# The scheduler's model behind a 2-layer hybrid backbone kernel: default model against timeline model

## The chip, the cores and the metric

The kernel runs on one NeuronCore of one Trainium2 chip. The metric is the device time of one execution in microseconds (us). Before the change it is 2091.67 us, the median of three runs (2090.68, 2091.67 and 2097.0 us). One further execution was profiled. Engines are called TensorE (PE in the profile, PEld for its weight loads), VectorE (DVE), ScalarE (ACT), GpSimd (POOL) and SyncE (SP, which only issues DMAs).

## The reference

Two layers work on 512 latent tokens and 256 context tokens of width 1024, all in float32.

```
for layer in range(2):
    h, hc = modulate(rms_norm(x), ...), modulate(rms_norm(ctx), ...)
    layer 0: y, yc = even_mixer(...)   # 8 heads global attention (2 kv heads, qk-norm, rotary)
                                       # + 8 heads sliding-window attention with a sink; then @ w_out
    layer 1: y = odd_mixer(...)        # 8 heads 2-D neighbourhood attention with a position bias
                                       # + 8 heads RWKV-7 in both directions; then @ w_out
    x = x + g1 * y;   x = x + g2 * swiglu(modulate(rms_norm(x), ...))
    ctx gets the same after layer 0 only
return rms_norm(x)
```

The RWKV-7 part is a recurrence over tokens, `S = S * w - (S kk) (kk a)^T + v k^T`, read out as `S r`. Its initial state comes from running the same recurrence over the context tokens. The feed-forward width is 2816.

## The kernel before, in words

**Tiling.** Features lie on the 128 partitions, tokens along the free dimension. Every projection keeps float32 accuracy by three passes (`mm3`, L387 to L389): each weight tile arrives by a DMA issued on SyncE (`wraw`, L133, 512 KB), ScalarE rounds it into `whi` (L143), VectorE or, in some stages, GpSimd subtracts to get `wlo` (L145), and TensorE multiplies high by high, high by low and low by high, 24 matmuls of 512 columns for one 128x1024 weight tile against the latent tokens.

**Stages in order of time.** Layer 0's input projection (`even_in`, `even_q`), its attention (`attend` and `pair`, L587 to L667) with the context's output projection and feed-forward beside it (`ctx_rest`), then layer 0's output projection and feed-forward for the latent tokens (`onto`, `ffn`) with layer 1's context part beside them (`ctx_chain`), then layer 1. Layer 1 begins with its projections (`odd_qkv` with L978 to L998, `shift_tile` with L1102 to L1109), beside which the RWKV operands are prepared (`prepare`). Each piece of `prepare` is a chain over ScalarE, VectorE and TensorE (`rwkv_elem`, L1188 to L1230), and each of its two groups ends with a 32x32 triangular inverse on VectorE (`rwkv_inverse`): four transposes of 32x1024 (L1255), 31 elimination steps (L1259, L1262), four transposes back (L1267). The recurrence then runs in chunks of 32 tokens, both directions together (`rwkv_step`, L1311 to L1351), with the rest of `prepare` and, later, the neighbourhood attention (`odd_pair`, L1047 to L1071) beside it. Layer 1's feed-forward (L387 to L389, L420, L712, L713) and the last norm (L1672) close the kernel.

**What sets the order.** Python generators (`aside`, `step`) interleave a main and a side stream when the program is traced; constants such as `B1`, `L1` or `F1` say how many side steps go with one main step. That gives each instruction a place in the traced program, and this place is its priority (`high_priority` in `attend` and `odd_pair` moves the score matmuls `QK_AHEAD` = 30 places forward). When the TileContext closes, the scheduler plays the program through on a model of the machine: whenever an engine is free in the model, it takes the instruction of lowest place among those whose inputs and buffers are ready in the model. The order so found is fixed in the program. On the chip each engine takes its own instructions in just this order, and a semaphore wait at the head of an engine's list holds all that stands behind it. Which buffer of a pool a tile gets, and the order of DMA issues on SyncE and GpSimd, come out of the same play. Nothing of the model is left in the program but the order, the buffers and the waits that follow from them.

In the program before, VectorE has 92% of its instructions at another place than the traced one, ScalarE 87%, SyncE 83%, GpSimd 74% and TensorE 57%; in the last eighth of TensorE's instructions the order is the traced one throughout.

The functions around the change:

## Time and profile before

| what | value |
|---|---|
| median of three runs | 2091.67 us |
| profiled execution, its own time | 2095.34 us |
| its span, first to last instruction | 2093.4 us |
| TensorE busy | 1981.8 us (95%) |
| VectorE busy | 1229.4 us (59%) |
| ScalarE busy | 893.1 us (43%) |
| GpSimd busy | 247.4 us (12%) |
| mean granted TensorE clock | 0.967 |
| DMA moved | 272.66 MB, 130 GB/s |

Busy time is the union of an engine's records. Matmuls overlap in the pipeline, so a TensorE that is always busy may still be doing little per microsecond; the granted clock says at which share of its full speed it ran. A row of the waits names the waiting instruction, the instruction that released it, the total in us, how often, and the longest one. A row of the timeline gives start, duration, engine, line, operation, output and inputs, and in brackets the idle time just before it with what ended it. A row of the stages gives the stretch, its length, busy us and number of instructions for TensorE's matmuls, its weight loads, VectorE, ScalarE and GpSimd, then the granted clock, the busy share of the DMA engines and GB/s.

### The profile page before, as it was taken

What the parts mean: (1) busy time and instruction counts of PE and PEld (TensorE: products, weight loads), DVE (VectorE), ACT (ScalarE), POOL (GpSimd) and SP (SyncE); (2) the same over time, 40 slices, a digit from 0 to 9 for tenths busy, and PEclk for the clock granted to TensorE, in tenths of its full rate; (3) what the DMA queues carried; (4) which work ended last, traced back from release to release, by engine and by line L of the source; (5) the groups of instructions that cost most, each with busy time, mean ns of one, the idle gap of its engine ahead of it and who ended that gap; (6) DMA issues with size and microseconds to landing.
All of it is one profiled execution on the core that took longest, in us unless ns stands there. A gap on an engine that the chain in (4) does not pass through costs nothing.

```text
span 2093.4 us, 38293 instructions
## 1 busy us (share of the span) xinstructions
PE 1981.8 (95%) x15556; PEld 1611.0 (77%) x15556; DVE 1229.4 (59%) x2407; ACT 893.1 (43%) x1682; POOL 247.4 (12%) x366
## 2 busy tenths in 40 slices
PE   6999999999988999999999999889899989999997
PEld 4766778999986888787777776667667768888887
DVE  5756676666666443559445655775766774333335
ACT  3335557775733433552222355535345443222222
POOL 1111100000000010000112132322322120000000
PEclk9999999999999999999999998988889999999999
DMA  7353322444484445433434323455675133232321
GB/s 272 124 200 122 142 91 81 142 126 127 135 271 160 151 156 151 140 108 107 146 102 132 111 71 92 123 158 161 162 222 144 33 121 101 92 101 91 101 92 49
DMA packets 112655, 272.66 MB, mean 130 GB/s; under 512 B 15424, under 2 KB 48736, under 8 KB 110944
## 3 DMA queue, kind: packets, MB, share of 16 engines
q1 hardware_dynamic: 100256, 224.74, 34.4%
q0 software_dynamic: 12224, 45.49, 6.6%
q8 instruction: 122, 2.00, 0.4%
q14 instruction: 53, 0.43, 0.1%
HBM read 238.20 MB, written 31.98 MB: 129 GB/s over the span
## 4 chain that ended last, share of the span: by engine, by line
PE 74%; DVE 11%; issue 9%; DMA 2%; ACT 2%; POOL 1%; SPq 0%; DVEq 0%; POOLq 0%; ACTq 0%
PE ps_b L387 16%; PE ps_b L389 16%; PE ps_b L388 16%; PE ps_v L637 4%; PE ps_a L587 2%; PE ps_e L609 2%; PE ps_w L1311 2%; PE ps_w L1317 2%; PE ps_s L1340 1%; DVE kb L1262 1%; PE ps_w L1330 1%; DVE kb L1255 1%; DVE pi L1259 1%; PE ps_a L1047 1%; PE ps_e L1218 1%
## 5 line engine op out<-in xcount | busy, mean ns | idle before, releaser
L143 ACT CAST whi<-wraw 128x1024 fp32r<-128x1024 f32 (+2 forms) x291 | 292.7, 1008 | 669.8 <-PE ps_b L388 509.4
L145 DVE TENSOR_TENSOR wlo<-wraw,whi 128x1024 fp32r<-128x1024 f32 (+2 forms) x251 | 296.1, 1180 | 213.5 <-ACT whi L143 207.5
L387 PE MATMUL ps_b<-hxh,whi 128*128 128x512 f32 (+1 forms) x1040 | 402.4, 390 | 13.0 <-ACT cj L978 7.2
L388 PE MATMUL ps_b<-hxl,whi 128*128 128x512 f32 (+1 forms) x1040 | 397.8, 385 | 1.6 <-DVE hxl L380 1.5
L389 PE MATMUL ps_b<-hxh,wlo 128*128 128x512 f32 (+1 forms) x1040 | 397.3, 384 | 0.3 <-DVE wlo L145 0.2
L387 PEld LDWEIGHTS ps_b<-hxh,whi 128*128 128x128 f32 x1040 | 198.6, 192 | 60.6 <-ACT cj L978 7.8
L388 PEld LDWEIGHTS ps_b<-hxl,whi 128*128 128x128 f32 x1040 | 199.0, 192 | 40.1 <-DVE hxl L380 3.0
L389 PEld LDWEIGHTS ps_b<-hxh,wlo 128*128 128x128 f32 x1040 | 198.7, 192 | 39.6 <-DVE wlo L145 1.3
L387 PE MATMUL ps_b<-act,whi 128*128 128x512 f32 (+1 forms) x570 | 200.5, 352 | 4.6 <-ACT whi L143 2.8
L389 PE MATMUL ps_b<-act,wlo 128*128 128x512 f32 (+1 forms) x570 | 197.0, 346 | 1.5 <-DVE wlo L145 1.5
L388 PE MATMUL ps_b<-act,whi 128*128 128x512 f32 (+1 forms) x570 | 196.7, 345 | 0.6 <-DVE act L124 0.6
L387 PE MATMUL ps_b<-hch,whi 128*128 128x256 f32 x552 | 159.6, 289 | 0.1
L389 PE MATMUL ps_b<-hch,wlo 128*128 128x256 f32 x552 | 156.2, 284 | 0.4 <-DVE wlo L145 0.4
L388 PE MATMUL ps_b<-hcl,whi 128*128 128x256 f32 x552 | 155.9, 283 | 0.0
L387 PEld LDWEIGHTS ps_b<-act,whi 128*128 128x128 f32 x570 | 109.5, 192 | 22.7 <-issue 5.5
L389 PEld LDWEIGHTS ps_b<-act,wlo 128*128 128x128 f32 x570 | 109.6, 192 | 15.0 <-DVE wlo L145 2.1
L388 PEld LDWEIGHTS ps_b<-act,whi 128*128 128x128 f32 x570 | 109.6, 192 | 12.9 <-DVE act L124 1.0
L420 DVE SCALAR_TENSOR_TENSOR xx<-ps_b,mod,xx 128x512 f32<-128x512 f32 (+1 forms) x64 | 43.7, 684 | 120.6 <-PE ps_b L389 119.3
L145 POOL TENSOR_TENSOR wlo<-wraw,whi 128x1024 fp32r<-128x1024 f32 (+1 forms) x40 | 88.5, 2217 | 204.6 <-ACT whi L143 180.0
L713 DVE TENSOR_TENSOR ff_a<-ff_a,ps_b 128x512 f32<-128x512 f32 x44 | 30.2, 687 | 134.3 <-PE ps_b L389 133.6
L387 PEld LDWEIGHTS ps_b<-hch,whi 128*128 128x128 f32 x552 | 104.7, 190 | 5.7 <-issue 2.5
L389 PEld LDWEIGHTS ps_b<-hch,wlo 128*128 128x128 f32 x552 | 104.4, 190 | 1.7 <-DVE wlo L145 1.4
(373 smaller groups left out, 3470.6 us busy)
## 6 DMA issues: line engine op xcount, KB each, us to landing
wraw<-in_ffi SPq DMA_DIRECT2D x132, 512.0 KB, 3.5
xx<-in_wmod POOLq DMA_DIRECT2D x48, 512.0 KB, 5.0
wraw<-in_w1in SPq DMA_DIRECT2D x43, 512.0 KB, 3.6
wraw<-in_ffo SPq DMA_DIRECT2D x48, 448.0 KB, 3.3
wmod<-in_wmod POOLq DMA_DIRECT2D x32, 512.0 KB, 4.8
wraw<-in_ffo SPq DMA_DIRECT2D x24, 512.0 KB, 3.5
op<-op SPq DMA_DIRECT2D x32, 384.0 KB, 4.2
qx<-in_wmod SPq DMA_DIRECT2D x16, 512.0 KB, 6.7
```

The costliest lines, as they stand in the source:

```text
L143: self.nc.scalar.copy(hi[:, 0:n], raw)
L145: e.tensor_tensor(lo[:, 0:n], raw, hi[:, 0:n].bitcast(F32), op=ALU.subtract)
L387: mm(out, lhsT=wh, rhs=hh, start=first, stop=False)
L388: mm(out, lhsT=wh, rhs=hl, start=False, stop=False)
L389: mm(out, lhsT=wl, rhs=hh, start=False, stop=last)
L420: self.nc.vector.scalar_tensor_tensor(X[:, m, c], ps[:, 0:n][:, c], gate[:, m, i : i + 1], X[:, m, c], op0=ALU.mult, op1=ALU.add)
L587: nc.tensor.matmul(o, lhsT=q, rhs=k[:, b : b + o.shape[1]], start=i == 0, stop=i == len(passes) - 1)
L609: nc.tensor.transpose(pt[:, P * (j - c) : P * (j - c) + P], p[:, P * j : P * j + P], self.ident)
L637: self.nc.tensor.matmul(ps[HD * u : HD * u + HD, col : col + P], lhsT=vs[u][j], rhs=pts[u][:, j, :], start=j == 0, stop=j == nk - 1, tile_ ...
L713: V.tensor_tensor(a, a, pg[1][:, 0:w], op=ALU.mult)
L1311: mm(wy[HD * u + HD - W_ + r : HD * u + HD, p, :], lhsT=G[top[u], p, r:W_], rhs=VU[top[u], p, u, :], start=p == 0, stop=False, skip_group_ ...
L1317: mm(o, lhsT=AR[:, p, :], rhs=Sd[:, p, u, :], start=False, stop=not lat, skip_group_check=True)
```

## The change

The TileContext is opened with `schedule_with_timeline_sim=True`. The play through the program then runs on the timeline model, in which each instruction is a list of timed events that take and free devices (sequencers, engines, their queues, DMA engines), in place of the default model. The traced program, its places, the buffers' sizes and the work of every instruction stay as they are; what may differ is the order on every engine and on every DMA queue, the buffer that a tile gets, and the waits.

```
-    with tile.TileContext(nc) as tc:
+    with tile.TileContext(nc, schedule_with_timeline_sim=True) as tc:
         with ExitStack() as ctx:
             Net(ctx, tc, ins, out).run()
```

## The prediction

> **What bounds the kernel now.** I read the page first, then the stages, then TensorE's waits in the worst stage, then the timeline around the three longest of them.
>
> ```profile
> span 2093.4 us, 38293 instructions
> PE 1981.8 (95%) x15556; PEld 1611.0 (77%) x15556; DVE 1229.4 (59%) x2407; ACT 893.1 (43%) x1682; POOL 247.4 (12%) x366
> ```
>
> TensorE is the bound: 2093.4 - 1981.8 = 111.6 us of its span are idle, and no other engine passes 59%. An order changes no instruction's work, so what can move is this idle time, and the time in which TensorE runs at a lower clock. The stages say where both lie (stretch, length, busy us of PE, PEld, DVE, ACT, POOL, granted clock, DMA share, GB/s):
>
> ```profile
> 0.00:50.00 50.00, 30.06 (x271) 21.63 (x272) 25.66 (x62) 18.33 (x34) 5.92 (x8) 0.93 0.79 284
> 50.00:300.00 250.00, 239.07 (x2128) 178.94 (x2127) 163.50 (x422) 115.48 (x290) 36.91 (x62) 0.99 0.40 138
> 300.00:560.00 260.00, 258.42 (x2254) 242.85 (x2253) 177.37 (x376) 180.89 (x366) 4.95 (x5) 1.00 0.37 117
> 560.00:700.00 140.00, 127.52 (x853) 110.74 (x854) 88.31 (x194) 55.52 (x93) 10.73 (x26) 0.94 0.63 208
> 700.00:1150.00 450.00, 445.69 (x3097) 354.55 (x3095) 230.85 (x356) 161.54 (x256) 37.58 (x78) 1.00 0.42 131
> 1150.00:1560.00 410.00, 367.53 (x3629) 283.57 (x3625) 280.90 (x544) 181.81 (x354) 114.36 (x141) 0.89 0.46 135
> 1560.00:1680.00 120.00, 118.44 (x1437) 87.00 (x1433) 84.08 (x184) 57.84 (x131) 22.94 (x38) 1.00 0.39 105
> 1680.00:1750.00 70.00, 62.96 (x358) 53.64 (x359) 49.08 (x98) 34.21 (x56) 13.97 (x10) 0.95 0.34 106
> 1750.00:2060.00 310.00, 310.00 (x1369) 256.68 (x1369) 110.27 (x119) 82.65 (x101) 0.00 (x0) 1.00 0.29 92
> 2060.00:2093.40 33.40, 22.11 (x181) 21.38 (x179) 19.34 (x57) 4.79 (x10) 0.00 (x0) 0.89 0.19 63
> ```
>
> Three kinds of stage. The first 50 us (19.94 idle) and the last 33.4 us (11.29 idle) are start and end, with little to choose from. The stages 300 to 560, 700 to 1150, 1560 to 1680 and 1750 to 2060 are full: 1.58 + 4.31 + 1.56 + 0 = 7.45 us idle in 1140, so a new order can only lose there. The stage from 1150 to 1560, where layer 1's projections and the RWKV work are interleaved, holds 410 - 367.53 = 42.47 us idle, and its clock of 0.89 stands for another (1 - 0.89) x 410 = 45.1 us, or 45.1 x 367.53 / 410 = 40.4 us on the busy part. That is where an order can win. What ends TensorE's waits there:
>
> ```profile
> PE ps_b L387 <- ACT cj L978: 7.2, 3, 5.2
> PE ps_e L1218 <- DVE kb L1202: 7.0, 1, 7.0
> PE ps_e L1227 <- DVE G L1222: 7.0, 6, 2.2
> PE ps_a L1047 <- DVE sm_m L1052: 5.0, 1, 5.0
> ```
>
> The longest single waits of rows one, two and four (5.15, 7.01 and 4.98 us, 17.14 in all) can be taken apart in the timeline. The first:
>
> ```profile
> 1347.28 0.50 ACT L1196 ACTIVATE KA<-th,half 128x256 f32<-128x256 f32 x1
> 1350.98 0.42 ACT L1200 ACTIVATE P<-sg 128x256 f32<-128x256 f32 x1 [3.20 <-DVE sg L1197]
> ...
> 1354.92 0.42 ACT L1200 ACTIVATE P<-sg 128x256 f32<-128x256 f32 x1 [1.52 <-DVE sg L1197]
> 1355.25 1.09 ACT L978 ACTIVATE cj<-ps_b 128x512 f32<-128x512 f32 x1
> ...
> 1356.39 0.80 PE L387 MATMUL ps_b<-hxh,whi 128*128 128x512 f32 x1 [5.15 <-ACT cj L978]
> ```
>
> ScalarE's order has two exponentials (L1200) ahead of the eviction L978. Both wait for VectorE's scan, 3.20 and 1.52 us, and L978, whose matmuls were over by 1356.39 - 5.15 = 1351.24, waits behind them, and TensorE for its bank. The order fits a play in which the scan comes sooner than on the chip. The second:
>
> ```profile
> 1383.64 7.67 DVE L1267 STREAM_TRANSPOSE G<-kb 32x1024 f32<-32x1024 f32 x4
> 1385.55 2.35 POOL L145 TENSOR_TENSOR wlo<-wraw,whi 128x1024 fp32r<-128x1024 f32 x1 [6.44 <-ACT whi L143]
> 1384.58 0.49 PE L387 MATMUL ps_b<-hxh,whi 128*128 128x512 f32 x1 [1.19 <-ACT cj L998]
> 1392.09 1.97 PE L1218 MATMUL ps_e<-AR,kb 64*64 64x64 f32 x32 [7.01 <-DVE kb L1202]
> 1394.76 0.77 PE L388 MATMUL ps_b<-hxl,whi 128*128 128x512 f32 x1
> ```
>
> TensorE's order has L1218 behind the first of 24 matmuls of a projection. L1218 needs L1202, which sits behind four transposes of 7.67 us; the other 23 matmuls, whose last operand `wlo` is there at 1385.55 + 2.35 = 1387.90, stand behind L1218 until 1394.76. This too fits a play with shorter transposes. The third:
>
> ```profile
> 1522.30 7.69 DVE L1267 STREAM_TRANSPOSE G<-kb 32x1024 f32<-32x1024 f32 x4
> 1530.02 0.42 DVE L1341 TENSOR_TENSOR S<-ps_s,S 128x256 f32<-128x256 f32 x1
> 1531.26 1.19 PE L1047 MATMUL ps_a<-ck,cq 128*128 128x512 f32 x2 [4.98 <-DVE sm_m L1052]
> ```
>
> Here everything hangs on VectorE, which again runs four transposes in one piece; recurrence (L1341) and attention (L1052) both wait for it.
>
> **The change, part by part.** It adds and removes no work. It gives every engine and DMA queue another order.
>
> *What a nearer model recovers.* If the new play has VectorE's times about right, the first wait shrinks to L978's own 1.09 us (5.15 - 1.09 = 4.06 saved), the second to 1387.90 - 1385.08 = 2.82 us (the wait began 7.01 before 1392.09; 4.19 saved). The third stays: the transposes come ahead by their place in the program, which no model alters. So (4.06 + 4.19 + 0) / 17.14 = 0.48 of what I could take apart. For the stage: 0.48 x 42.47 = 20.4 us. Bounds: nothing, if the timeline model misses the same durations, and all 42.47.
>
> *The clock.* A long wait is paid twice:
>
> ```profile
> 1357.84 0.63 PE L387 MATMUL ps_b<-hxh,whi 128*128 128x512 f32 x1
> 1362.62 0.39 PE L387 MATMUL ps_b<-hxh,whi 128*128 128x512 f32 x1
> ```
>
> After the first wait matmuls took 0.63 us, five us later 0.39. Of the 40.4 us I take half of the share of the idle time, 40.4 x 0.48 / 2 = 9.7 us, since a wait cut to 2.8 us need not spare the slow stretch behind it. Bounds 0 and 40.4.
>
> *What the new order loses elsewhere.* The full stages are where the present order happens to keep TensorE fed. The nearest row for an ordinary interleaved stage is that from 50 to 300, with 10.93 idle in 250, or 4.4%. I put this on the two stages where attention interleaves with something else: 0.044 x 260 - 1.58 = 9.8 and 0.044 x 120 - 1.56 = 3.7, together 13.5 us. Not on 700 to 1150 and 1750 to 2060: there TensorE has dense projections whose order leaves little choice. What covers these is the work of ScalarE and VectorE done ahead (both under 71% busy in 300 to 560); without cover the price is that of 1150 to 1560, 42.47 / 410 = 10.4% idle and 11% of clock on 260 us, or 27 - 1.6 + 28.6 = 54. Bounds 0 and 54.
>
> *ScalarE's table loads* move with the order as well.
>
> ```profile
> L712 ACT ACT_TABLE_LOAD x15 | 19.2, 1283 | 1.5 <-PE ps_b L389 1.2
> L599 ACT ACT_TABLE_LOAD x14 | 18.0, 1283 | 0.2
> L712 ACT ACTIVATE xx<-ps_b 128x256 f32<-128x256 f32 x22 | 8.4, 382 | 0.2
> ```
>
> From 300 to 560 the context's 22 Silu alternate with the attention's Exp, at 15 + 14 loads of 1.283 us. Every Silu in a gap of its own would make 44 loads, 15 more, or 19.2 us of ScalarE, which has 260 - 180.89 = 79.1 us idle there. I cost this at nothing, with 0 to 19.2 as bounds. The Trainium skill, ScalarE: Activation LUTs, section "Table sets: the hidden batching unit", asks that calls be batched by set, against which an order by readiness goes; its section "What ACT_TABLE_LOAD costs" gives about 2.66 us for a switch with its drain. By that figure the 15 would be an estimated 40 us, still inside the idle time, and the sum would be the same.
>
> *Sum.* 2095.3 (the profiled execution; its span and 1.9 us around it) - 20.4 - 9.7 + 13.5 = 2078.7; the profiled execution is 3.7 above the median, so **2075 us**, 0.8% below the median.
>
> **The rivals.**
>
> *Slower: the attention stage comes apart.* Place: 300 to 560. TensorE there takes score matmuls, transposes and value matmuls that each wait for a softmax step, among the context's projections; if the new play believes a softmax step early, TensorE stands before a transpose with projections ready behind it, as at L1218 above. Price: half of the 54 us, 27, while nothing is recovered from 1150 to 1560. 2095.3 + 27 - 3.7 = 2119 us. It decides from the point where it costs more than the recovered 30. For it: 0.6% idle is little to start from. Against it: nothing in this stage takes as long on VectorE as the transposes.
>
> *Slower: SyncE's queue.* Stores wait in it for their data:
>
> ```profile
> SPq L1486 <- ACT KT L1223: 39.5, 9, 8.2
> ```
>
> ```profile
> wraw<-in_w1in SPq DMA_DIRECT2D x43, 512.0 KB, 3.6
> L143 ACT CAST whi<-wraw 128x1024 fp32r<-128x1024 f32 (+2 forms) x291 | 292.7, 1008 | 669.8 <-PE ps_b L388 509.4
> ```
>
> If the new order puts a weight fetch straight behind such a store, the weight is late by up to 8.2 us. Two weights in hand cover 2 x 24 matmuls at 310 / 1369 = 0.226 us each (the stage from 1750), 10.9 us; the wait, the landing, the rounding and GpSimd's subtraction take 8.2 + 3.6 + 1.0 + 2.4 = 15.2. So up to 4.3 us late, nine times, 39 us; half of it is 19, with nothing recovered: 2095.3 + 19 - 3.7 = 2111 us. Against it: today's order has the same queue and waits of this kind do not show on TensorE.
>
> *No change.* The orders differ, but where TensorE is full they make no difference and in 1150 to 1560 VectorE's long transposes hold in any order; 2092 us.
>
> **How the numbers follow.** Forecast 0.46, attention stage 0.27, SyncE 0.10, no change 0.17. A measurement of this kernel tells about 0.3% (6 us) from no change. That makes 0.46 faster, 0.17 the same, 0.37 slower. The forecast's own range is 2040 (all of 0.48 of both terms recovered, 39.8, and half of the 12.5 idle from 560 to 700 and 8.4 of clock, with no loss: 2095.3 - 39.8 - 10.5 - 3.7 = 2041) to 2085. With the other side taken in, and the attention stage at up to three quarters of its full price (2132), the range is 2040 to 2133.
>
> **What would show it.** Right: from 1150 to 1560 the idle time falls to about 22 us, the clock rises above 0.91, L978 no longer stands behind L1200, and the projection's matmuls run during the transposes. The losses show as idle time over 3 us in 300 to 560 and 1560 to 1680. Wrong: idle time from 1150 to 1560 at 42 us or above with the same waits for L1202 and L978, which would say that the timeline model is no nearer there; or TensorE's waits for Exp or for `sm_t` from 300 to 560 at more than 15 us.

## The result and the profile after

The kernel with the timeline model's order takes 2180.07 us (median of four runs, 2176.28 to 2183.54), the kernel before 2092.16 us beside it: a ratio of 1.0416 with a 95% interval of 1.039 to 1.0442, or 88 us slower. The prediction said 2075 us, with a range from 2040 to 2133.

The page of the kernel after, first lines:

```profile
span 2179.8 us, 38326 instructions
PE 2023.5 (93%) x15556; PEld 1644.5 (75%) x15556; DVE 1219.6 (56%) x2407; ACT 898.4 (41%) x1684; POOL 242.1 (11%) x366
```

TensorE has the same 15556 instructions. It sits idle for 2179.8 - 2023.5 = 156.3 us, 44.7 more than before, and is busy 2023.5 - 1981.8 = 41.7 us longer with the same work. About half of the loss is thus no idle time at all. The mean granted clock fell from 0.967 to 0.949. The clock's records in the two traces are either full or half, and TensorE is busy at half clock for 110.8 us before and for 170.8 us after. If a busy microsecond at half clock loses half at most, the clock accounts, as an estimate from these figures, for at most 30 of the 41.7 us; the other 12 or more are something else.

The stretches of the kernel after, at the cuts used before (length, busy us of PE, PEld, DVE, ACT, POOL, granted clock, DMA share, GB/s). Since the work falls behind more and more, a stretch holds somewhat earlier work than the stretch of the same times before:

```profile
50.00:300.00 250.00, 226.45 (x1969) 171.01 (x1963) 144.78 (x386) 102.51 (x258) 32.83 (x60) 0.95 0.36 126
300.00:560.00 260.00, 255.28 (x2087) 229.00 (x2088) 170.50 (x373) 167.90 (x352) 4.48 (x6) 0.99 0.33 107
560.00:700.00 140.00, 131.27 (x879) 115.41 (x879) 76.77 (x144) 59.03 (x95) 6.92 (x17) 0.94 0.57 191
700.00:1150.00 450.00, 431.21 (x2753) 340.09 (x2753) 228.55 (x389) 167.40 (x267) 27.91 (x65) 0.98 0.43 134
1150.00:1560.00 410.00, 378.08 (x3251) 299.90 (x3251) 256.02 (x470) 176.37 (x316) 104.51 (x124) 0.90 0.38 113
1560.00:1680.00 120.00, 105.98 (x1535) 81.10 (x1533) 86.76 (x195) 56.05 (x134) 27.21 (x51) 0.86 0.66 185
```

The stages that were full are no longer so: 700 to 1150 has 18.79 us idle where 4.31 were, 50 to 300 has 23.55 where 10.93 were.

Where the loss arises is read better from the same work in both traces. The rows below are lines of TensorE with their first and last start, first of the kernel before:

```profile
L587 PE MATMUL ps_a<-kst,qc x64: 276/362/388, 181.1 to 273.9; 128*128 128x256 f32 x64
L637 PE MATMUL ps_v<-sm_t,vt x800: 272/273/324, 186.1 to 572.8; 128*64 128x128 f32 x160
L1150 PE MATMUL ps_e<-c_blk,cj x32: 170/251/272, 1221.5 to 1250.6; 128*128 128x2 f32 x32
L1349 PE MATMUL ps_w<-VU,op x512: 214/219/316, 1407.7 to 1650.7; 128*32 128x64 f32 x128, 32*32 32x64 f32 x43
```

and of the kernel after:

```profile
L587 PE MATMUL ps_a<-kst,qc x64: 274/282/581, 196.7 to 294.7; 128*128 128x256 f32 x64
L637 PE MATMUL ps_v<-sm_t,vt x800: 272/273/476, 201.2 to 606.8; 128*64 128x128 f32 x160
L1150 PE MATMUL ps_e<-c_blk,cj x32: 165/251/252, 1289.3 to 1319.4; 128*128 128x2 f32 x32
L1349 PE MATMUL ps_w<-VU,op x512: 213/219/317, 1487.9 to 1742.8; 128*32 128x64 f32 x128, 32*32 32x64 f32 x43
```

The first attention score comes 15.6 us later, the last value product of layer 0 34.0, the first L1150 67.8, the last recurrence step (L1349) 92.1, and the end 86.4. The loss is not in one place: it grows from milestone to milestone up to the end of the recurrence, and shrinks by some 6 us behind it.

How far an order overtakes can be counted in the program: the lead of an instruction is the number of places it stands ahead of the oldest instruction of its engine that has not been issued. On TensorE the mean lead is 16.5 before and 63.1 after (largest 1059 and 2301), on VectorE 6.9 and 14.0, on ScalarE 3.2 and 8.8. One weight tile is 24 matmuls.

### The profile page after: what moved, and what is told of

Its sections match the earlier page's. It is cut to its first block, busy times and chain, and to the rows that moved or that the text cites. A ratio compares the mean times of both kernels' runs of the same rounds, so it can differ in the third digit from the quotient of the medians.

```text
span 2179.8 us, 38326 instructions
## 1 busy us (share of the span) xinstructions
PE 2023.5 (93%) x15556; PEld 1644.5 (75%) x15556; DVE 1219.6 (56%) x2407; ACT 898.4 (41%) x1684; POOL 242.1 (11%) x366
## 4 chain that ended last, share of the span: by engine, by line
PE 78%; DVE 8%; DMA 5%; issue 5%; ACT 3%; SPq 0%; POOL 0%; DVEq 0%; ACTq 0%; POOLq 0%
PE ps_b L387 16%; PE ps_b L389 16%; PE ps_b L388 16%; PE ps_v L637 4%; PE ps_a L587 2%; PE ps_e L609 2%; DMA xx<-in_wmod 2%; PE ps_s L1340 1%; PE ps_w L1311 1%; PE ps_b L465 1%; PE ps_w L1317 1%; PE ps_b L467 1%; PE ps_b L466 1%; PE ps_e L1218 1%; DMA wmod<-in_wmod 1%
## 5 line engine op out<-in xcount | busy, mean ns | idle before, releaser
L145 POOL TENSOR_TENSOR wlo<-wraw,whi 128x1024 fp32r<-128x1024 f32 (+1 forms) x40 | 88.0, 2205 | 177.7 <-ACT whi L143 156.3
L388 PEld LDWEIGHTS ps_b<-hcl,whi 128*128 128x128 f32 x552 | 104.2, 189 | 0.7 <-DVE ps_a L590 0.2
```

The costliest lines, as they stand in the source:

```text
L145: e.tensor_tensor(lo[:, 0:n], raw, hi[:, 0:n].bitcast(F32), op=ALU.subtract)
L388: mm(out, lhsT=wh, rhs=hl, start=False, stop=False)
```

## The experiments

The orders are exchanged in this way: the program is built once with one model, its order is read, and a second build with either model gets edges without semaphores between neighbours of one engine, which bind chosen engines (or places) to that order. The core of all experiments, with `build` holding what `kernel` did before:

```diff
+    def build(timeline, hold=None, engines=(), part=None, lead=None):
...
+        with tile.TileContext(nc, schedule_with_timeline_sim=timeline) as tc:
...
+                for i in hold:
+                    e = str(insts[i].engine).split(".")[-1]
+                    if e in engines and (part is None or part(i, mark)):
+                        if e in last:
+                            tc.add_manual_dep(insts[i], insts[last[e]].name, info, reason="held order")
+                        last[e] = i
+    _, hold = build(False)
```

Below, ALL stands for the five engines' names. The expectations name the theories by letters; A is that the far overtaking itself costs, the others are said where they come up.

**Is it the order at all?** The timeline play with the default's order on all engines:

```diff
+    nc, _ = build(True, hold, ALL)
```

> The timeline play, with the instructions of all five engines bound to the order that the default play gives (edges without a semaphore between neighbours of one engine). Only the buffers that tiles get and the waits may still differ from the kernel before. Theory A (the loss lies in the order) and theory B (the same, but in the order of VectorE and ScalarE): 2092 us within 10. Theory C (the loss lies in buffers, waits and what follows from them): above 2130 us.

2098.47 us beside 2094.06, ratio 1.002 (1.0002 to 1.0038). The order makes the loss; what else the other play could change (buffers, waits), together with the binding edges, is worth at most 0.4%.

**Which engine's order?** The default's order on TensorE alone, then on VectorE and ScalarE alone, each with the timeline play for the rest; then the reverse, the default play with TensorE held to the timeline's order:

```diff
+    nc, _ = build(True, hold, ("PE",))
+    nc, _ = build(True, hold, ("DVE", "Activation"))
+    _, hold = build(True)
+    nc, _ = build(False, hold, ("PE",))
```

> The timeline play, TensorE alone bound to the default order; the other engines and the DMA queues are ordered by the timeline play around it. Theory A (TensorE takes the side stream's dense matmuls too early and has none left to cover the chains): most of the 88 us come back, 2090 to 2115 us. Theory B (VectorE's and ScalarE's own orders delay the chains): little comes back, above 2150 us.

> The timeline play, VectorE and ScalarE bound to the default order, TensorE, GpSimd and the queues free. Theory A: the dense matmuls still run early where their inputs allow it, above 2140 us. Theory B: 2090 to 2115 us. If both engines only follow one another (bound evictions and roundings hold TensorE's matmuls back as well), both e2 and e3 come back.

> The reverse of the second: the default play, TensorE alone bound to the order that the timeline play gives. Theory A: most of the loss appears, 2150 to 2190 us. Theory B: little of it, 2090 to 2120 us.

Ratios 1.03 (1.0185 to 1.0415), 1.0546 (1.0489 to 1.0602) and 1.0546 (1.0479 to 1.0613); 2157.23, 2208.7 and 2208.79 us. The default's order on TensorE alone gives back some 23 of the 88 us (two executions, 18 us apart), and the two other mixtures are slower than the timeline's order whole. By the letter of the expectations the first speaks for theory B, the second for theory A, and the third lies beyond both. The question was put wrongly: these mixtures show that one engine's order can't be judged beside orders of the other engines that it was not made with.

**Which layer?** The default's order held for layer 0's places, then for layer 1's:

```diff
+    nc, _ = build(True, hold, ALL, lambda i, mark: i < mark)
+    nc, _ = build(True, hold, ALL, lambda i, mark: i >= mark)
```

> The timeline play; all engines bound to the default order for what is traced before layer 1 is called (layer 0 with layer 1's context part), free behind it. If the loss is a sum over stages as the matmuls' progress in the two traces says (68 us behind by the first matmul of layer 1's key norm, L1150, 88 at the end): about 2092 + 20 = 2112 us. If one stage's order carries the loss of the other: below 2100 or above 2135 us.

> The reverse: layer 0 free, all engines bound to the default order from layer 1's call on. Sum over stages: about 2092 + 68 = 2160 us. If layer 1's share was only a consequence of layer 0's order: 2180 us.

2116.65 us, ratio 1.0116 (1.0087 to 1.0146), and 2162.12 us, ratio 1.0334 (1.0286 to 1.0382), beside 2092.58. Layer 1 in the timeline's order costs 24 us and layer 0 costs 70; together 94, against 88 for both. Within these intervals the losses add.

**Is far overtaking what costs?** A bound on the lead: block b of an engine's instructions, in traced order, may issue only when all of block b - 2 has.

```diff
+    nc, _ = build(True, lead={"PE": 48, "DVE": 12, "Activation": 6})
+    nc, _ = build(True, lead={"PE": 150, "DVE": 30, "Activation": 20})
```

> The timeline play with a bound on how far an instruction may overtake earlier traced ones of its own engine: 48 to 96 places on TensorE (two to four weight tiles), 12 to 24 on VectorE, 6 to 12 on ScalarE. Theory A (far overtaking costs): most comes back, 2095 to 2125 us. Theory D (the play's beliefs at short range cost, a wait at the head of the line, and overtaking only fills gaps): as slow as the changed kernel or slower, 2180 us or more.

> The same with a bound of 150 to 300 places on TensorE, 30 to 60 on VectorE, 20 to 40 on ScalarE. Theory A: between the short bound and the changed kernel, 2110 to 2160 us. Theory D: within 10 us of the changed kernel's 2180.

2241.74 us, ratio 1.0714 (1.0683 to 1.0745), and 2173.77 us, ratio 1.0389 (1.0359 to 1.042). At first this seemed to end theory A. The control shows that it doesn't: the same bounds on the default play.

```diff
+    nc, _ = build(False, lead={"PE": 48, "DVE": 12, "Activation": 6})
+    nc, _ = build(False, lead={"PE": 150, "DVE": 30, "Activation": 20})
```

> Control for the short bound: the default play with the same bounds on the lead (48 on TensorE, 12 on VectorE, 6 on ScalarE). It tells whether the bound itself or the timeline play under the bound made the 2242 us. Theory D (the two plays believe different things ready at short range, and the timeline play's beliefs fit the chip worse): 2090 to 2120 us, since the default play overtakes little and the bound takes little from it. Theory A' (the block bound itself costs, whatever the play): 2150 us or more.

> Control for the long bound: the default play with 150, 30 and 20. Theory D: 2085 to 2100 us. Theory A' (the bound itself costs): 2120 us or more.

2239.32 us, ratio 1.0697 (1.0677 to 1.0716), and 2119.94 us, ratio 1.013 (1.0099 to 1.016). Of the two theories in these expectations, D is out and A' holds (the long bound just at the edge of its range): the bound itself costs the default play 146 and 27 us, so it is no clean test of theory A. What the four experiments do show: some overtaking is needed (forbidding it costs more than the whole change), and the two plays differ by 2 us under the short bound, 54 under the long one and 88 without a bound. The difference lies in what the timeline play does with its freedom to overtake.

**The traced places or the play?** The constants of the interleaving were set with the default play. If they mislead the timeline play, it should do better with the default's own order as its places:

```diff
+            def instruction_hook(self, instruction):
...
+                    self.cur_priority = places[len(here[0].instructions)]
...
+    nc, _ = build(True, places=[nth.get(i, i) for i in range(len(first) + 4000)])
```

> The timeline play, but each instruction's place is its rank in the default play's order instead of its traced place. In this play an instruction leaves that order only where the model believes its inputs or buffers late. Theory D (beliefs on what is ready): the order stays far from the default's, and the time stays within 10 us of 2180. Theory F (the traced places, tuned by hand to the default play, mislead the timeline play): 2095 to 2130 us, since the places are now the good order itself.

2175.71 us, ratio 1.0373 (1.0345 to 1.0401). Its TensorE still stands at another place than the default's order in 9409 of 12030 instructions; with the traced places it is 9449. So the places are not the cause; since the play takes the lowest place that is ready, it must take other instructions to be ready. Which of the model's durations are to blame is not shown by any run.

**The prediction's own two waits.** The default's order with L978 ahead of the two exponentials on ScalarE, and the other 23 matmuls of the projection tile ahead of the products L1218 on TensorE:

```diff
+    hold.remove(acts[k])
+    hold.insert(hold.index(acts[to]), acts[k])
...
+    moved = [i for i in pes[k:] if line[i] in (387, 388, 389)][:23]
...
+    at = hold.index(pes[k])
+    hold[at:at] = moved
+    nc, *_ = build(False, hold, ALL)
```

> The default play's order with the two edits that the prediction priced: ScalarE's L978 ahead of the two exponentials, and the other 23 matmuls of the projection tile ahead of the 16 products L1218. The prediction's first term: 4.06 + 4.19 us saved, and up to as much again in clock, so 2076 to 2084 us. Rival (the 23 matmuls are the cover of later waits, those of L1227 and of the recurrence, and are missing there): within 0.2% of the kernel before or slower, 2088 to 2100 us, with new waits of several us for L1222 and L1202 behind the moved tile.

2090.81 us beside 2093.43, ratio 0.9994 (0.9974 to 1.0015): no difference that can be measured. The two waits did go for the most part. TensorE's two waits, and the stretches around them, first of the kernel before and then of this one:

```profile
1348.95 0.50 PE L387 MATMUL ps_b<-hxh,whi 128*128 128x512 f32 x1 [0.76 <-ACT cj L978]
1389.38 1.15 PE L1218 MATMUL ps_e<-AR,kb 64*64 64x64 f32 x32 [2.07 <-DVE kb L1202]
```

```profile
1340.00:1365.00 25.00, 19.85 (x78) 14.98 (x78) 24.19 (x49) 10.20 (x19) 4.76 (x2) 0.86 0.48 136
1365.00:1382.00 17.00, 15.49 (x71) 12.63 (x70) 16.18 (x27) 7.17 (x8) 7.45 (x3) 1.00 0.47 144
1382.00:1400.00 18.00, 9.66 (x92) 7.25 (x91) 12.27 (x17) 4.80 (x10) 2.35 (x1) 0.72 0.63 207
1400.00:1450.00 50.00, 48.76 (x687) 35.39 (x687) 32.62 (x68) 29.49 (x66) 13.91 (x20) 0.87 0.47 129
```

```profile
1340.00:1365.00 25.00, 22.84 (x102) 17.42 (x101) 24.15 (x49) 12.71 (x21) 8.17 (x3) 1.00 0.39 108
1365.00:1382.00 17.00, 10.60 (x41) 7.88 (x40) 16.01 (x32) 6.08 (x8) 4.98 (x2) 0.80 0.46 139
1382.00:1400.00 18.00, 15.11 (x148) 11.73 (x148) 13.09 (x18) 5.59 (x13) 2.40 (x1) 0.81 0.65 210
1400.00:1450.00 50.00, 50.00 (x676) 37.64 (x673) 32.81 (x67) 30.48 (x67) 14.38 (x21) 0.73 0.50 134
```

The waits shrank from 5.15 to 0.76 and from 7.01 to 2.07 us, 9.33 together, a little more than predicted. About half of that came back at once as idle time elsewhere: from 1340 to 1450 TensorE is idle for 16.24 us before and 11.45 here. The stretch from 1365 has 6.40 us idle where it had 1.51, and the longest wait that is left for L978 is 4.7 us:

```profile
PE ps_b L387 <- ACT cj L978: 6.3, 3, 4.7
```

VectorE is busy for 40.16 of the first 42 us, as before (40.37), which fits a piece that it bounds, but no run here varies VectorE's work. The rival in the expectation has the time right and not the mechanism: the waits for L1222 and L1202 did not grow. And the other half was no loss in the execution that was profiled: its last L1188 starts 5.9 us earlier than before and its span is 5.8 us shorter (2087.6 to 2093.4). The twelve executions scatter from 2080 to 2106 us, the lowest with a clock of 0.970, the highest with 0.961, and their median is only 2.6 us lower. So the runs exclude the expected 2076 to 2084 us; a gain of up to 5 us they leave open.

**One part at a time.** The timeline play's order for one range of places, the default's for all others: up to the first attention score; from there to the last value product; from there to layer 1; and from layer 1's first neighbourhood score to the end.

```diff
+    nc, *_ = build(True, hold, ALL, lambda i, mark: i >= scores)
+    nc, *_ = build(True, hold, ALL, lambda i, mark: not scores <= i < onto)
+    nc, *_ = build(True, hold, ALL, lambda i, mark: not onto <= i < mark)
+    nc, *_ = build(True, hold, ALL, lambda i, mark: i < tail)
```

> The default order is held on every engine from the first attention score's place on; the input stage before it (modulation, input projection) comes from the timeline play. Its TensorE order takes the modulation's products (L224) 32 at a time and the projection's in runs of 20 and more, where the default order takes 8 and 4 or 5 in turn; the last seven groups of 32 have no projection left between them. Theory G (the side work is used up early, and the stage's own loss of 15.6 us at the first score stays to the end): 2104 to 2114 us, with the clock under 0.9 from 150 to 200 us. Theory H (the shift at the first score is made good later, where the order behind is the default's): 2090 to 2098 us.

> Only the attention of layer 0, with the context's rest beside it (places from the first score to the last value product), comes from the timeline play. By the milestones of the two traces it lost 34 - 15.6 = 18 us there. Theory G: 2106 to 2118 us. Theory H: within 6 us of 2092.

> Only the places from the end of layer 0's attention to the beginning of layer 1 (output projection, feed-forward, layer 1's context part) come from the timeline play. By the milestones it lost 67.7 - 34 = 34 us there. Theory G: 2118 to 2132 us, and the three parts' losses add up to 60 to 80 us. Theory H, or a loss made by one place alone: one of the three has nearly all of the 70 us and the others are within 8 us of 2092.

> The default order is held up to layer 1's first neighbourhood-attention score; the rest (attention, end of the recurrence, output projection, feed-forward) comes from the timeline play. By the milestones the timeline order gained some 6 to 10 us between the recurrence's end and the end. If that was a better order: 2083 to 2089 us, faster than both kernels. If it was only work pulled ahead of a late recurrence: 2090 to 2104 us.

Beside 2094.12 us:

| Part in the timeline's order | us | ratio (95%) | loss, us | idle, span's | busy, span's |
|---|---|---|---|---|---|
| input stage | 2111.11 | 1.0076 (1.0059 to 1.0093) | 17.0 | +14.3 | +3.8 |
| attention of layer 0 | 2116.96 | 1.0108 (1.0091 to 1.0125) | 22.8 | +8.4 | +13.6 |
| rest of layer 0 | 2127.95 | 1.0153 (1.0132 to 1.0173) | 33.8 | +13.7 | +20.8 |
| tail of layer 1 | 2115.58 | 1.0106 (1.0083 to 1.0128) | 21.5 | +20.4 | -10.6 |

(The last two columns are TensorE's idle and busy time in the profiled execution against that of the kernel before.) The three parts of layer 0 add up to 73.6 us, against 70 for layer 0 as a whole. All three lie in theory G's ranges, so the milestones were a fair map, and nothing is made good later. The tail, which I hoped was better, is worse, above both ranges of its expectation. Its profiled execution (span 2103.2) was also its best; the times go from 2105 at a clock of 0.966 to 2125 at 0.961, and why the clock varies so is open. Layer 1 as a whole lost 24 us, its tail alone 21.5: as far as losses add, the rest of layer 1, where the prediction saw its gain, comes out within 3 us of the kernel before. The tail's longest waits of its own:

```profile
PE ps_b L339 <- DVE rms0y L113: 8.6, 3, 5.6
PE ps_w L1311 <- DMA op<-op: 6.0, 2, 5.5
PE ps_g L1380 <- DVE Yd L1373: 4.5, 1, 4.5
```

The columns say that the input stage loses by idle time and the attention mostly by busy time. That asks for two mechanisms.

**Cover used up early (input stage).** Cover is work of another stream that TensorE can do while a transfer is under way. From 150 to 200 us, before, after, and with the input stage alone:

```profile
150.00:200.00 50.00, 47.02 (x431) 34.22 (x429) 31.51 (x74) 24.84 (x61) 6.71 (x13) 1.00 0.37 127
```

```profile
150.00:200.00 50.00, 35.88 (x415) 25.05 (x414) 18.56 (x43) 13.74 (x28) 11.35 (x22) 0.77 0.71 252
```

```profile
150.00:200.00 50.00, 36.38 (x428) 25.50 (x427) 20.24 (x48) 15.62 (x36) 10.50 (x20) 0.83 0.70 248
```

Both orders have the same transfers of modulation weights and the same projection. The default's order takes the modulation's products (L224) 8 at a time, mostly with 4 or 5 projection matmuls between, and most transfers land under these. The timeline's order takes 32 products at a time and up to 24 projection matmuls at once beside them. The projection's last matmuls, before and after (first and last start):

```profile
L467 PE MATMUL ps_b<-whi,hcl x48: 390/396/500, 37.7 to 180.0; 128*128 128x512 f32 x48
```

```profile
L467 PE MATMUL ps_b<-whi,hcl x48: 390/394/628, 40.0 to 158.8; 128*128 128x512 f32 x48
```

They run out 21 us earlier, and the last products stand bare before their transfers:

```profile
178.14 1.95 PE L224 MATMUL ps_t<-xx,silu_c 128*32 128x128 f32 x64
180.48 0.33 PE L238 MATMUL ps_t<-ident,xc 128*128 128x128 f32 x1 [0.39 <-ACT xc L234]
183.41 0.64 PE L224 MATMUL ps_t<-xx,silu_c 128*32 128x128 f32 x16 [2.61 <-DMA xx<-in_wmod]
184.57 1.08 PE L224 MATMUL ps_t<-xx,silu_c 128*32 128x128 f32 x16 [0.51 <-DMA xx<-in_wmod]
```

This cause by itself, on the default's order: 47 projection matmuls go ahead of the last 96 products.

```diff
+    at = [k for k in range(end) if line[pes[k]] == 224][-96]
+    moved = [i for i in pes[at:end] if line[i] in (465, 466, 467)]
+    rest = [i for i in pes[at:end] if line[i] not in (465, 466, 467)]
+    pe = iter(pes[:at] + moved + rest + pes[end:])
```

> The default order held on every engine, with one edit on TensorE: the 47 projection matmuls (L465 to L467) that stand among the last 96 modulation products (L224) before the first score go ahead of these. It takes 47 x 0.235 = 11.0 us of cover away from the last transfers of the modulation's weights. If cover is what the input stage loses: TensorE's waits for in_wmod grow by 5 to 11 us (3.2 us before) and the time by as much, 2097 to 2104 us. If the transfers come in time anyway while the projection runs: 2092 to 2095 us.

2103.43 us beside 2094.81, ratio 1.0042 (1.0025 to 1.0059). TensorE's wait for the weights, before and here, and the stretch:

```profile
PE ps_t L224 <- DMA xx<-in_wmod: 3.2, 4, 1.1
PE ps_t L224 <- DMA xx<-in_wmod: 9.2, 8, 2.4
150.00:200.00 50.00, 40.04 (x352) 30.13 (x351) 23.41 (x52) 16.65 (x39) 6.31 (x12) 0.86 0.36 127
```

The wait was 3.2 us before and is 9.2; 6.98 us more lie idle from 150 to 200 and the clock falls to 0.86. Moving 47 matmuls, with none added, costs 8.6 us. That is half of the 17.0 us of the input stage, where the same wait is 10.0 us and the clock lower still; the other half has no experiment of its own.

**More changes of kind (attention).** Value products, transposes and scores are three kinds of small matmuls; a run is a series of one kind without another between. With the attention alone TensorE is busy for 13.6 us more, and the busy time of its value products grows by 13.8. (A group's busy time is the union of its own records, and groups overlap: that of the transposes L609 grows by 4.0 at the same time and that of the scores L587 falls by 9.4, so groups don't add up to the whole.) TensorE's group L637 before, after, with the attention alone, and in the last experiment (busy us, mean ns):

```profile
L637 PE MATMUL ps_v<-sm_t,vt 128*64 128x128 f32 x800 | 69.8, 282 | 1.6 <-DVE sm_t L611 1.6
```

```profile
L637 PE MATMUL ps_v<-sm_t,vt 128*64 128x128 f32 x800 | 83.6, 288 | 1.1 <-DVE sm_t L611 0.8 <-ACT sm_t L611 0.2
```

```profile
L637 PE MATMUL ps_v<-sm_t,vt 128*64 128x128 f32 x800 | 83.6, 288 | 1.4 <-DVE sm_t L611 1.1 <-ACT sm_t L611 0.2
```

```profile
L637 PE MATMUL ps_v<-sm_t,vt 128*64 128x128 f32 x800 | 77.7, 287 | 1.4 <-DVE sm_t L611 1.4
```

A single product takes about as long in all of them; they overlap less. It isn't the clock, which is 0.970 with the attention alone and 0.967 before; TensorE is busy at half clock for 99.6 us there and 110.8 before. In the program the products L637 stand in 119 runs before and 156 after (30 of them layer 1's each time); in the trace of before, the last product of a run holds TensorE 0.19 us until the next kind starts, one inside a run 0.06 on average. This cause by itself, on the default's order: runs of products and the run of transposes or scores behind them are taken in turn, piece by piece, 151 runs in all.

```diff
+        if line[a[0]] == 637 and len(a) >= 4 and b and line[b[0]] in (587, 609) and len(b) >= 2 and scores <= a[0] < onto:
+            n = min(len(a) // 2, len(b))
+            for j in range(n):
+                new += a[len(a) * j // n : len(a) * (j + 1) // n] + b[len(b) * j // n : len(b) * (j + 1) // n]
```

> The default order held on every engine, with one edit on TensorE: in the attention of layer 0 a run of value products (L637) and the run of transposes (L609) or scores (L587) behind it are cut into pieces and taken in turn, which makes 151 runs of L637 in place of 119 (the timeline order has 156). The last product of a run takes 0.19 us to the next kind, one inside a run 0.06. If the changes of kind are what the attention loses: the busy time of L637 rises from 69.8 to some 76 to 84 us with the clock as before, and the time is 2098 to 2110 us. If not: L637 stays under 73 us and the time within 4 us of 2092.

2109.41 us beside 2094.81, ratio 1.0081 (1.0058 to 1.0104), with the clock at 0.970. TensorE's first lines of the pages of before, of the attention alone and of this kernel:

```profile
PE 1981.8 (95%) x15556; PEld 1611.0 (77%) x15556; DVE 1229.4 (59%) x2407; ACT 893.1 (43%) x1682; POOL 247.4 (12%) x366
PE 1995.4 (94%) x15556; PEld 1611.0 (76%) x15556; DVE 1229.5 (58%) x2407; ACT 894.0 (42%) x1682; POOL 245.7 (12%) x366
PE 1988.8 (95%) x15556; PEld 1608.1 (76%) x15556; DVE 1230.4 (59%) x2407; ACT 893.5 (42%) x1682; POOL 247.3 (12%) x366
```

The products' busy time rises by 7.9 us, that of the transposes L609 from 65.5 to 70.7, and TensorE's whole by 7.0, with only 2.1 us more idle. The profiled execution is 9.1 us longer than before's and the shortest of six; the median is 14.6 longer. The 32 further runs at 0.19 - 0.06 = 0.13 us would be 4.2. So the mechanism is shown, its price per change only roughly, and it makes 7.0 of the 13.6 us with nearly as many runs as the timeline's order has. What it is in a change of kind that costs isn't tested: the products' weights are 128x64, those of the transposes and scores 128x128.

## Why the prediction was wrong, step by step

Between the forecast and the result lie 105 us. Taking the two gains as nothing, some 30 of them are these gains, and the other 75 are the term for losses: 13.5 us in the sum, 88 on the chip.

**"What can move is this idle time, and the time in which TensorE runs at a lower clock."** This premise failed. With the attention alone in the timeline's order, busy time grew by 13.6 us at the same clock, about half of it by more changes between kinds of small matmuls. In the whole kernel busy time is 41.7 us of the loss, of which the clock has 30 at most.

**"What a nearer model recovers", 20.4 us.** Two steps failed. The first is that the timeline play would remove the two waits: it did not. The second is the 0.48, by which a wait removed was idle time gained, and which was carried over to the whole stage. The sizes of the two waits were right (8.25 predicted, 9.33 found when both were removed), but about half came back as idle time near by, and of the rest the medians show no gain that can be told from noise. I read who ended each wait and not that VectorE was busy nearly throughout around them. After, the same two waits stand at

```profile
1450.95 0.80 PE L387 MATMUL ps_b<-hxh,whi 128*128 128x512 f32 x1 [5.32 <-ACT cj L978]
1469.79 1.97 PE L1218 MATMUL ps_e<-AR,kb 64*64 64x64 f32 x32 [4.48 <-DVE kb L1202]
```

and L978 is now behind a weight cast that is late, no longer behind L1200:

```profile
1448.85 1.04 ACT L143 CAST whi<-wraw 128x1024 fp32r<-128x1024 f32 x1 [7.15 <-DMA wraw<-in_w1in]
1449.80 1.09 ACT L978 ACTIVATE cj<-ps_b 128x512 f32<-128x512 f32 x1
```

The third wait, which was to stay, is gone: L1047 no longer waits for L1052, though VectorE still runs four transposes in one piece for 7.7 us. TensorE's longest wait around the recurrence is another one, 8.0 us of L1311 for a transfer of `op`.

Of the signs under "What would show it", idle time from 1150 to 1560 fell from 42.47 to 31.92, about half of the way to 22, the clock came to 0.90 and not above 0.91, and L978 left L1200. The signs of loss came in full: 4.72 us idle from 300 to 560 and 14.02 from 1560 to 1680. Yet layer 1 in the timeline's order lost 24 us: a stretch of fixed times was a poor witness, because other work had moved into it.

**The clock, -9.7 us.** Wrong sign: 0.967 became 0.949. The forecast had let a wait be paid twice, once as idle time and once in the clock, and had used this for the waits that go and not for those that come.

**"What the new order loses elsewhere", 13.5 us.** This is the step that decided. It put the loss on two stages alone and at nothing in the others, and it was far too small: 17 us in the input stage, which I left out; 23 in the attention, where I had put 9.8; 34 in the rest of layer 0, which includes 700 to 1150, where I put nothing on the ground that dense projections leave little choice. There the part alone has 9.40 us idle against 4.31, and 19.40 against 12.48 from 560 to 700:

```profile
560.00:700.00 140.00, 120.60 (x812) 100.85 (x812) 82.73 (x186) 48.73 (x81) 13.26 (x29) 0.93 0.63 207
700.00:1150.00 450.00, 440.60 (x2830) 347.67 (x2829) 216.39 (x334) 161.72 (x251) 28.87 (x62) 0.99 0.41 126
```

What its 20.8 us of busy time consist of I have not taken apart; busy time at half clock is 17.3 us longer than before, so at most some 9 of them are the clock's. The cause of this largest part stays open, and so does that of the tail, which lost 21 more, where the term had 3.7. I had written that in the full stages "a new order can only lose"; I should have charged that to all of them, since each part lost 0.8 to 1.5% of the whole.

**Table loads at nothing.** Nothing speaks against it: 43 loads after, 41 before, and ScalarE is 41% busy.

**The rivals.** The attention stage did come apart, for 22.8 us beside the 27 I gave it, but mostly not by waits, as I had it: 8.4 us are idle time, with 4.7 for `sm_y` in L609 (1.0 before), and 13.6 busy time. As a rival of one place it was still far off, because three other parts lost as much. SyncE's queue was not tested alone; the late weight above is a case of its kind, since its fetch was issued at 1445.05, straight behind four stores (L961) that had held the queue from 1438.63, waiting 4.4 and 2.6 us for their data. What such cases cost in sum is not shown. That the change makes no difference is excluded.

## What to carry to other kernels

A program that is kept busy by a hand-set interleaving has its cover in the order itself. Here another scheduling model didn't repair the worst stage and leave the others alone: it reordered all of them, and each of the four parts that were tested lost. Before counting a wait as gain, see which engine is busy throughout the piece around it, and expect part of the wait to come back elsewhere. And an order is to be read for two things beside waits: whether side work still stands next to the transfers it covers, and how often TensorE changes from one kind of small matmul to another.

## What was not expected of the hardware

A change of kind among small matmuls has a price that isn't the clock's: 32 more runs of value products among scores and transposes made 7.9 us more busy time in these products, and the kernel 0.81% slower. And the clock falls without any long wait: after, the stretch from 150 to 200 us has no idle time of TensorE above 2.6 us in one piece, but 14.1 in all, most of it in thirteen waits for transfers,

```profile
PE ps_t L224 <- DMA xx<-in_wmod: 9.4, 13, 2.6
```

and a granted clock of 0.77. With the 47 matmuls moved, the stretch has 10.0 us idle, at most 2.4 in one piece, and a clock of 0.86; before it is 3.0 and 1.00. The Trainium skill, "TensorE: Matmul & The Clock Gate", section "HAM oscillation — how this bites in real kernels", tells of the same thing, matmul work in pieces between waits for transfers losing its clock, but sets the limit at pauses above some 3.4 us. The traces agree with the first and go further than the second.
